# Three of eight chunks of an attention output projection's second half as seven block products instead of eight

## The chip, the cores and the metric

The kernel runs on one core of one Trainium2 chip. The core has a matrix engine (TensorE, PE in the profile, with its weight loads in a row of their own, PEld), a vector engine (VectorE, DVE), a scalar engine (ScalarE, ACT), GpSimd (POOL) and SyncE (SP), which here only issues transfers. On-chip memory is SBUF; matrix products go to PSUM, which has eight banks of 128x512 float32 values. The metric is the device time of one execution in microseconds (us).

## The reference

The reference is a two-layer encoder for 256 positions of width 2048. Layer 0 mixes tokens with a gated MLP, layer 1 with latent attention; behind each mixer stands a gated MLP with a short convolution. After each of the four, `x = LayerNorm(ALPHA * x + sublayer(x))`. What matters here is the end of the attention:

```python
    k_nope, v = jnp.split(kv, [NOPE_DIM], axis=-1)
    o = chunk_causal_attention(q_nope, q_rope, k_nope, k_rope, v)
    return o.reshape(B, S, MLA_HEADS * V_DIM) @ w_out
```

Sixteen heads give `o` of 256x2048, and `w_out` is 2048x2048. The result is added to the layer's input and normalised, and the last gated MLP (`x @ w_up`, 2048 to 11008) follows.

## The kernel before

**Products of split numbers.** Every float32 operand is split into a high part, which the matrix engine takes as it is, and a low part, the rest. A block product of a 128x128 block of activations and a 128x512 block of weights is then three matmuls: high by high, low by high, high by low (`prod_b`, L359). The high part of a weight chunk is a cast on ScalarE (L125), the low part a subtraction on VectorE (L128).

**The feed.** `Feed` (L77) streams all weights in chunks of 128x2048 (1 MB) in the order of their use: one load on SP into one of three "raw" slots (`_load`, L88), the split (`_split`, L104), and then the products. `feed.next(splits, loads)` hands over the next chunk and writes down the splits of the next two or three chunks and the loads of two more. The split parts lie in 14 "big" slots of 128x2048 words, which also hold the residual (2 slots), the heads' outputs `oT` (4 slots, one for four heads) and, before, the keys. Six "side" slots hold the split queries (4) and the values (2) during the attention. Small tiles rotate through five slots "t2".

**Order.** The program is written in one order; a scheduler at compile time puts the instructions of each engine into a fixed order. It goes by the written order among those that are ready in its own model, and a tile gets a slot when one is free. An engine then runs its list in order.

**Eight and seven block products.** A chunk holds two blocks of 128 rows of the weights (j = 0, 1) by two column blocks of 512 (f = 0, 1), and the activations have two row blocks (b = 0, 1): eight block products, 24 matmuls. Many stages of the kernel do some of their chunks in another way: a form of Strassen's method with seven block products, 21 matmuls. It needs sums of the four weight blocks, sums of the four activation blocks, and a last combination of the accumulators:

- `_seven` (L131) splits such a chunk. It forms four running sums `ts` of the weight blocks with three additions on VectorE (L139, L140, L142), and splits both the weights (`wh`, `wl`, 1536 columns) and the sums (`th`, `tl`, 1536 and 512 columns). It takes five slots where the other form takes two. From chunk 96 on, which holds here, the next cast on ScalarE is ordered behind the last cast of the sums (`self.sums`).
- `combine` (L296) forms the four sums of the activations with four subtractions or additions (`turn`, L288), one cast and one subtraction (L302, L303).
- `Banks.seven` (L435) issues the seven products, three into the accumulators of the plain form (`DIRECT`) and four into banks of their own (`OWN`). A stage with such chunks needs eight banks.
- `Banks.rest` (L445) combines the own banks after the last seven chunk with one copy on ScalarE and four operations on VectorE; `ln.fold` (L655) then adds the four results to the residual, scaled by ALPHA. A later `ln.piece` (L661) adds the plain accumulators.

**The stretch around the change.** The attention runs head by head (`attend_a`: scores and softmax; `attend_b`: transposed probabilities; `attend_c`, L1174: output of a head, split into `oT`), interleaved with the first half (columns 0 to 1023) of the output projection, `mo0`. Four pieces of the residual and their statistics follow (L1230 to L1232). Then comes the second half, `mo1` (L1233 to L1245): eight chunks c = 0 to 7, all with eight products into four banks. The products of the last three chunks are put off (`SKEW`, `late`) and issued bank by bank in `end_mo` (L1247). `boundary` (L555) does that: after the two column blocks of b = 0 are done, it takes their pieces and the statistics, scales the residual and has PE transpose it (`ln.put`, L713) while PE still works at b = 1; the transposed and split residual `xhl` feeds the first products of the next gated MLP, `upf`.

Of the kernel before, what the change touches and what calls it, by code (L numbers as in the profile page):

```python
# [9 lines left out]
F32R = mybir.dt.float32r  # L10
# [5 lines left out]
P = 128  # L16
S = 256
# [27 lines left out]
SKEW = 3  # L45
# [5 lines left out]

U_PAIRS = [[0, 1, 5, 7, 2, 6, 3, 4]] + [[0, 1, 2, 5, 3, 7, 4, 6]] * 5
U_SEVEN = [(2, 3)] + [(2, 3, 4)] * 4 + [(2, 3)]

T1, T2 = 6, 5
SLOTS = {"big": 14, "raw": 3, "side": 6}
# [153 lines left out]
def trunk(ctx: ExitStack, tc: tile.TileContext, x, xT, gm_in, gm_wout, ffn_up, ffn_dn,  # L210
          ml_q, ml_kv, ml_b, ml_out, consts, w_sT, b_s, ropes, ln_rows, out):
    nc = tc.nc
# [10 lines left out]
    def slot(shape, name, dt=F32, tag="big"):  # L223
        return big.tile(shape, dt, tag=tag, name=name, bufs=SLOTS[tag])

    def bank(name):
        return ps.tile([P, 512], F32, tag="bank", name=name)

    def mm(o, l, r, start, stop):
        recent[0] = nc.tensor.matmul(o, l, r, start=start, stop=stop, skip_group_check=True)  # L230
        return recent[0]
# [12 lines left out]
    chunks, parked = [], []  # L244
# [4 lines left out]
    for g in range(6):  # L249
        for p in U_PAIRS[g]:  # L250
            i = 48 + 8 * g + p // 2
            w = gm_in[i : i + 5 : 4, :, p % 2 * 1024 : p % 2 * 1024 + 1024].rearrange("f p c -> p f c")
            chunks.append((w, 2048, "seven" if p in U_SEVEN[g] else "wide"))

# [15 lines left out]
    chunks += [(ml_q[i], 2048, "") for i in range(4)]  # L270
    chunks += [(ml_kv[i], 3 * KVR, "") for i in range(5)] + [(ml_kv[5, :, 0:KVR], KVR, "")]
    chunks += [(ml_b[i], 2048, "") for i in range(ml_b.shape[0])]
    chunks += [(ml_out[i], 2048, "") for i in range(ml_out.shape[0])]
    chunks += [(ffn_up[1, i], 2048, "") for i in range(n_up)]
    back(ffn_dn[1], NF_FF)

# [1 line left out]
    feed = Feed(nc, tc.keep_in_program_order, behind, order, big, dram, chunks)  # L278
# [9 lines left out]
    def turn(t, k1, k2):  # L288

        at = lambda k, b: k[:, b] if len(k.shape) == 3 else k[:, b * P : (b + 1) * P]  # L290
        tc.keep_in_program_order(nc.vector.tensor_tensor(t[:, 0], at(k1, 0), at(k1, 1), ALU.subtract))
        nc.vector.tensor_tensor(t[:, 1], at(k1, 1), at(k2, 1), ALU.subtract)
        nc.vector.tensor_tensor(t[:, 2], t[:, 1], at(k1, 0), ALU.subtract)
        nc.vector.tensor_tensor(t[:, 3], at(k2, 0), t[:, 2], ALU.add)

    def combine(name, o, k1, k2):  # L296


        t = tp.tile([P, 4, P], F32, tag="t2", name=f"xs{name}", bufs=T2)
        turn(t, k1, k2)  # L300
        o = o.rearrange("p (h s c) -> p h s c", h=2, s=4)
        nc.scalar.copy(o[:, 0], t)  # L302
        nc.vector.tensor_tensor(o[:, 1], t, o[:, 0].bitcast(F32), ALU.subtract)  # L303
        return [(o[:, 0, i], o[:, 1, i]) for i in (1, 2, 0, 3)]

    for j in range(4):
        t = slot([P, 4, S], f"xraw{j}", tag="side")
# [47 lines left out]
    def x_parts(xs, k, b):  # L355
        t = xs[k // 4]
        return (t[:, k % 4, b * P : (b + 1) * P], t[:, k % 4, S + b * P : S + (b + 1) * P])

    def prod_b(acc, parts, hi, lo, pieces, first, last):  # L359

        xh, xl = parts
        for f, (o, w) in enumerate(pieces):
            mm(acc[f][:, :w], xh, hi[:, o : o + w], first, False)
            mm(acc[f][:, :w], xl, hi[:, o : o + w], False, False)
            mm(acc[f][:, :w], xh, lo[:, o : o + w], False, last)
# [37 lines left out]
    OWN, DIRECT = ("p1", "q5", "p7", "p6"), ("q3", "p2", "e", "q4")  # L403
# [327 lines left out]
    halfp = [(0, 512), (512, 512)]  # L731
# [19 lines left out]
    for gi in range(6):  # L751

        acc = Banks(f"v{gi}", DIRECT if gi == 0 else OWN + DIRECT if gi % 2 else DIRECT + OWN)
        rest = (None,) * 4
        for c, p in enumerate(V_PAIRS[gi]):
            a = [[x_parts(xhl, 2 * p + j, b) for j in range(2)] for b in range(2)]
            got = feed.next()
# [8 lines left out]
            if gi == 0 and p in V_SEVEN[1]:  # L766
                x4 = xraw[p // 2]
                room = xc_room[len(xc) // 2][:, len(xc) % 2, :]
# [8 lines left out]
            if c == 7 and gi == 5:  # L777
                wTg = []
                for i in range(4):
                    t = tp.tile([P, 2, P], F32, tag="t1", name=f"wT{i}", bufs=T1)  # L780
# [4 lines left out]
        for i, (n, t) in enumerate(zip(DIRECT, rest)):  # L785
            o = vt[:, i // 2, (i % 2) * 512 : (i % 2) * 512 + 512]
# [66 lines left out]
    def turned(g, tiles):  # L853

        for i, t in enumerate(tiles):
            src = v[g][:, i // 2, i % 2 * 512 : i % 2 * 512 + 512]
            for j in range(4):
                nc.tensor.transpose(t[:, j * P : (j + 1) * P], src[:, j * P : (j + 1) * P], ident)
            nc.scalar.copy(src, t)
# [7 lines left out]
    for g in range(6):  # L867
        direct, own = (ub[4:], ub[:4]) if g % 2 else (ub[:4], ub[4:])
        acc = Banks(f"u{g}", DIRECT + OWN, direct + own)
        for c, p in enumerate(U_PAIRS[g]):  # L870
            a = [[x_parts(xhl, 2 * p + j, b) for j in range(2)] for b in range(2)]
            got = feed.next()
            if p in U_SEVEN[g]:
                acc.seven(a, xc[p], *got, turned=512, across=True)
                if p == U_SEVEN[g][-1]:
                    rest = acc.rest()
# [17 lines left out]
        for i, t in enumerate(rest):  # L894
            o = v[g][:, i // 2, i % 2 * 512 : i % 2 * 512 + 512]
            nc.vector.tensor_tensor(o, o, t, ALU.mult)

    ln = Norm(0, {})
    acc, end = down(NF_GM, pT, "wo", ln, acts, tiles=ub, beside=lambda: turned(5, ub[4:]))
# [66 lines left out]
    ln, acc, end = ffn(0, ln, acc, end, False)  # L966
# [61 lines left out]
    acc = [[bank(f"mkv{b}_{f}") for f in range(2)] for b in range(2)]  # L1028
    for c in range(6):
        hi, lo = feed.next()  # L1030
        for j in range(3 if c < 5 else 1):
            k = 3 * c + j
# [9 lines left out]
    for b in range(2):  # L1042
# [3 lines left out]
        t = tp.tile([P, 4, ROPE], F32, tag="t1", name=f"kr2_{b}", bufs=T1)  # L1046
# [18 lines left out]
    acc = [[bank(f"qr{b}_{f}") for f in range(2)] for b in range(2)]  # L1065
    for c in range(2):
        hi, lo = feed.next()
        for j in range(2):
            k = 2 * c + j
# [52 lines left out]
    oT = []  # L1122
# [51 lines left out]
    def attend_c(h):  # L1174
        if h % 4 == 0:
            oT.append(slot([P, 4, 512], f"oT{h // 4}", F32R))
        pts = probs.pop(h)
        o = bank(f"o{h}")
        c = slice(h * P, (h + 1) * P)
        mm(o[:, 0:S], vv[0][:, c], pts[:, 0:S], True, False)  # L1180
        mm(o[:, P:S], vv[1][:, c], pts[:, S : 3 * P], False, True)
        hi = oT[h // 4][:, h % 4, 0:S]
        nc.scalar.copy(hi, o[:, 0:S])
        nc.vector.tensor_tensor(oT[h // 4][:, h % 4, S : 2 * S], o[:, 0:S], hi.bitcast(F32), ALU.subtract)

    for hf in range(2):
        acc = [[bank(f"vv{hf}_{b}_{f}") for f in range(2)] for b in range(2)]
        for c in range(2):
            hi, lo = feed.next()
            for j in range(2):  # L1190

                k = 2 * c + j
# [7 lines left out]
        for b in range(2):  # L1200
            for f in range(2):
                c = slice(hf * 1024 + f * 512, hf * 1024 + (f + 1) * 512)
                nc.scalar.copy(vv[b][:, c], acc[b][f])


    ln = Norm(2, res)
    acc = [[bank(f"mo0_{b}_{f}") for f in range(2)] for b in range(2)]
    LAG = 4
    attend_c(0)
    for t in range(3, H + LAG):  # L1210
        k = t - LAG
        if k >= 0:
            if k % 2 == 0:
                hi, lo = feed.next()
            w = slice((k % 2) * 1024, (k % 2) * 1024 + 1024)
        if 3 < t < H:
            attend_a(t)
        if k >= 0:
            prod_b(acc[0], x_parts(oT, k, 0), hi[:, w], lo[:, w], halfp, k == 0, k == KD - 1)
        if t < H + 2:  # L1220
            attend_c(t - 2)
        if k >= 0:
            prod_b(acc[1][:1], x_parts(oT, k, 1), hi[:, w], lo[:, w], halfp[:1], k == 0, k == KD - 1)
        if t - 1 < H:
            attend_b(t - 1)
        if k >= 0:
            prod_b(acc[1][1:], x_parts(oT, k, 1), hi[:, w], lo[:, w], halfp[1:], k == 0, k == KD - 1)
    ln.begin()
    ln.prep()
    for b in range(2):  # L1230
        for f in range(2):
            ln.piece(b, f, acc[b][f])  # L1232
    acc = [[bank(f"mo1_{b}_{f}") for f in range(2)] for b in range(2)]  # L1233
    late = []
    for c in range(8):
        left = 7 - c
        hi, lo = feed.next(splits=2 if left > 5 else 3, loads=2)
        for j in range(2):
            k = 2 * c + j
            w = slice(j * 1024, (j + 1) * 1024)  # L1240
            if left < SKEW:
                late.append((hi[:, w], lo[:, w], k))
                continue
            for b in range(2):
                prod_b(acc[b], x_parts(oT, k, b), hi[:, w], lo[:, w], halfp, k == 0, False)  # L1245

    def end_mo(b, f):  # L1247
        for hi, lo, k in late:
# [3 lines left out]
    ln, acc, end = ffn(1, ln, banks, end_mo, True)  # L1252
# [99 lines left out]
```

## Time and profile before

| | |
|---|---|
| time, median of 3 runs | 2465.37 us (2465.03 to 2466.1) |
| span of the profiled execution | 2464.6 us |
| matmuls of the output projection | 384 (256 with `wh`, 128 with `wl`) |
| attention with the first half of the projection | about 1637 to 1706 us of the span |
| second half of the projection | about 1706 to 1750 us |
| first products of the next gated MLP | from 1750.58 us |

The span counts from the first to the last instruction, and is 0.8 us below the median of the runs. In the profile, "busy" for PE counts pipelined matmuls, so PE at 100% says that it hardly ever waits, not that it runs at its peak. A group row of the profile gives line, engine, operation, output and inputs by tile name, sizes, count, then busy time and the mean of one in ns, and the idle time in front of them. A row of the timeline gives start, duration (both us), engine, line, operation, tiles and count; a bracket at its end gives the engine's idle time before it and what ended that.

### The profile page before, as it was taken

Reading aid. Unit: us, or ns where it says so; the run is one execution under the profiler, and the core shown is the slowest. Engines: PE = TensorE matmul, PEld = TensorE weight load, DVE = VectorE, ACT = ScalarE, POOL = GpSimd, SP = SyncE. Lnnn points to the kernel's source line nnn. Section 1 sums busy time; section 2 is a strip of 40 time slices with the busy share of each in tenths; the row PEclk is TensorE's granted clock in tenths of the full one; section 3 lists DMA queues with packets and bytes.
Section 4 is the critical chain, followed back from the end, with each engine's and each line's share of the span. In section 5 each row is a group of like instructions: output and inputs, shape, how many; then the busy total and the mean of one; then the engine's idle time right before and its main releaser. Section 6 shows DMA issues by size and latency. Waiting matters only on the chain. (4 is left out here: it accounts for less than half of the span.)

```text
span 2464.6 us, 32483 instructions
## 1 busy us (share of the span) xinstructions
PE 2458.1 (100%) x12494; PEld 2091.3 (85%) x12494; DVE 2054.7 (83%) x2734; ACT 1459.3 (59%) x1967; POOL 104.2 (4%) x202
## 2 busy tenths in 40 slices
PE   9999999999999999999999999999999999999999
PEld 7888888888888888888888888988888888888887
DVE  7999999989897788778777997867598787878798
ACT  6666665566565666656554566665565665555453
POOL 0000000000000000000001000000000000000000
PEclk9999999999999999999999999999999999999999
DMA  7555666656665778778868885544478787777885
GB/s 291 202 208 205 226 204 202 205 188 205 222 212 198 241 282 314 300 279 300 322 218 318 301 301 182 184 170 156 172 269 309 275 305 304 295 265 278 299 324 201
DMA packets 116428, 611.94 MB, mean 248 GB/s; under 512 B 10648, under 2 KB 10912, under 8 KB 75184
## 3 DMA queue, kind: packets, MB, share of 16 engines
q1 hardware_dynamic: 90128, 462.47, 52.9%
q0 software_dynamic: 26144, 147.39, 15.8%
q8 instruction: 98, 1.61, 0.3%
q14 instruction: 58, 0.48, 0.1%
HBM read 544.75 MB, written 65.06 MB: 247 GB/s over the span
## 5 line engine op out<-in xcount | busy, mean ns | idle before, releaser
L128 DVE TENSOR_TENSOR wl<-raw,wh 128x1024 fp32r<-128x1024 f32 (+4 forms) x645 | 958.4, 1501 | 169.5 <-ACT wh L125 124.0
L125 ACT CAST wh<-raw 128x1024 fp32r<-128x1024 f32 (+4 forms) x645 | 809.0, 1278 | 356.8 <-PE up L230 80.7
L230 PE MATMUL up<-xhl,wh 128*128 128x512 f32 x2624 | 611.4, 390 | 0.0
L230 PEld LDWEIGHTS up<-xhl,wh 128*128 128x128 f32 x2624 | 487.4, 188 | 97.8
L230 PEld LDWEIGHTS up<-xhl,wl 128*128 128x128 f32 x2624 | 325.8, 192 | 6.4
L230 PE MATMUL up<-xhl,wl 128*128 128x256 f32 x2624 | 328.1, 283 | 0.0
L125 ACT CAST th<-ts 128x1536 fp32r<-128x1536 f32 (+1 forms) x138 | 142.5, 1052 | 110.9 <-DVE ts L135 80.3
L230 PE MATMUL ub<-wh,xhl 128*128 128x512 f32 x576 | 179.5, 393 | 0.0
L128 DVE TENSOR_TENSOR tl<-ts,th 128x1536 fp32r<-128x1536 f32 (+1 forms) x138 | 163.2, 1221 | 10.4 <-PE dn_p L230 3.4
L230 PEld LDWEIGHTS ub<-wh,xhl 128*128 128x128 f32 x576 | 108.1, 188 | 24.2 <-issue 1.9
L230 PE MATMUL ub<-wl,xhl 128*128 128x512 f32 x288 | 112.1, 389 | 0.0
L135 DVE TENSOR_TENSOR ts<-ts,raw 128x512 f32<-128x512 f32 x138 | 95.1, 689 | 1.4
L135 DVE TENSOR_TENSOR ts<-raw 128x1024 f32<-128x1024 f32 x69 | 84.3, 1221 | 6.1 <-PE ub L230 3.8
L230 PE MATMUL mo<-wh,oT 128*128 128x512 f32 x256 | 82.5, 401 | 0.0
L230 PE MATMUL v_q<-wh,xhl 128*128 128x512 f32 x224 | 70.7, 391 | 0.3 <-ACT wh L125 0.3
L230 PEld LDWEIGHTS ub<-wl,xhl 128*128 128x128 f32 x288 | 54.1, 188 | 11.3
L230 PE MATMUL v_p<-wh,xhl 128*128 128x512 f32 x192 | 59.9, 389 | 0.0
L230 PEld LDWEIGHTS mo<-wh,oT 128*128 128x128 f32 x256 | 45.5, 189 | 7.1
L230 PEld LDWEIGHTS v_q<-wh,xhl 128*128 128x128 f32 x224 | 42.0, 188 | 10.5 <-ACT wh L125 1.9
L230 PE MATMUL mo<-wl,oT 128*128 128x512 f32 x128 | 50.1, 391 | 0.0
L724 ACT ACTIVATE lny<-lnt,lncol 128x128 f32<-128x128 f32 x96 | 36.6, 472 | 15.6 <-PE lnt L720 15.5
L388 DVE TENSOR_TENSOR h_0a<-up,lo_0a 128x256 f32<-128x256 f32 x41 | 17.2, 421 | 33.0 <-ACT lo_0a L386 33.0
(1838 smaller groups left out, 4338.4 us busy)
## 6 DMA issues: line engine op xcount, KB each, us to landing
raw<-in_ffn_up_dram SPq DMA_DIRECT2D x172, 1024.0 KB, 7.0
raw<-in_gm_in_dram SPq DMA_DIRECT2D x93, 1024.0 KB, 5.3
raw<-in_ffn_dn_dram SPq DMA_DIRECT2D x68, 1024.0 KB, 7.2
raw<-in_gm_wout_dram SPq DMA_DIRECT2D x48, 1024.0 KB, 5.3
praw<-in_ffn_dn_dram POOLq DMA_DIRECT2D x16, 1024.0 KB, 13.9
keptth<-pth POOLq DMA_DIRECT2D x16, 1024.0 KB, 8.1
kepttl<-ptl POOLq DMA_DIRECT2D x16, 1024.0 KB, 8.8
fth<-keptth POOLq DMA_DIRECT2D x16, 1024.0 KB, 9.4
```

The costliest lines, as they stand in the source:

```text
L125: cast = self.nc.scalar.copy(hi, raw)
L128: self.nc.vector.tensor_tensor(lo, raw, hi.bitcast(F32), ALU.subtract)
L135: add = lambda o, a, b: self.nc.vector.tensor_tensor(o, a, b, ALU.add)
L230: recent[0] = nc.tensor.matmul(o, l, r, start=start, stop=stop, skip_group_check=True)
L388: nc.vector.tensor_tensor(h, acc[:, 0:S], lo, ALU.add)
L724: nc.scalar.activation(y[:, j], t[:, j * P : (j + 1) * P], AF.Identity, bias=lncol[:, o : o + 1], scale=lncol[:, g : g + 1])
```

## The change

The attention's second half of the output projection takes the seven-product form for its chunks c = 2, 3 and 4.

```diff
+MO_SEVEN = (2, 3, 4)
...
-    chunks += [(ml_out[i], 2048, "") for i in range(ml_out.shape[0])]
+    chunks += [(ml_out[i], 2048, "seven" if i - ml_out.shape[0] // 2 in MO_SEVEN else "") for i in range(ml_out.shape[0])]
...
         hi = oT[h // 4][:, h % 4, 0:S]
         nc.scalar.copy(hi, o[:, 0:S])
         nc.vector.tensor_tensor(oT[h // 4][:, h % 4, S : 2 * S], o[:, 0:S], hi.bitcast(F32), ALU.subtract)
+        if h // 2 in MO_SEVEN:
+            if not oraw:
+                oraw["room"] = slot([P, 2 * len(MO_SEVEN), S], "oraw", tag="side")
+            oraw[h] = oraw["room"][:, h - 2 * MO_SEVEN[0], :]
+            nc.scalar.copy(oraw[h], o[:, 0:S])
+            if h % 2:
+                combine_o(h // 2)
...
+    oraw, osum = {}, {}
+
+    def combine_o(c):
+
+        if not osum:
+            room = slot([P, 2, 8 * P], f"os{c}", F32R, "side")
+            last = slot([P, 8 * P], f"ot{c}", F32R, "side")
+            osum["room"] = [room[:, 0, :], room[:, 1, :], last]
+        osum[c] = combine(f"o{c}", osum["room"][MO_SEVEN.index(c)], *[oraw.pop(2 * c + j) for j in range(2)])
...
-    acc = [[bank(f"mo1_{b}_{f}") for f in range(2)] for b in range(2)]
     late = []
+    second = Banks("mo1", DIRECT + OWN)
     for c in range(8):
         left = 7 - c
-        hi, lo = feed.next(splits=2 if left > 5 else 3, loads=2)
-        for j in range(2):
-            k = 2 * c + j
-            w = slice(j * 1024, (j + 1) * 1024)
-            if left < SKEW:
-                late.append((hi[:, w], lo[:, w], k))
-                continue
-            for b in range(2):
-                prod_b(acc[b], x_parts(oT, k, b), hi[:, w], lo[:, w], halfp, k == 0, False)
+        got = feed.next(splits=2 if left > 5 else 3, loads=2)
+        if left < SKEW:
+            for j in range(2):
+                w = slice(j * 1024, (j + 1) * 1024)
+                late.append((got[0][:, w], got[1][:, w], 2 * c + j))
+            continue
+        a = [[x_parts(oT, 2 * c + j, b) for j in range(2)] for b in range(2)]
+        if c in MO_SEVEN:
+            second.seven(a, osum[c], *got)
+            if c == MO_SEVEN[-1]:
+                for j, t in enumerate(second.rest()):
+                    ln.fold(j // 2, 2 + j % 2, t)
+        else:
+            second.eight(a, *got)
+    acc = [[second.acc[DIRECT[2 * b + f]] for f in range(2)] for b in range(2)]
```

So the heads 4 to 9 are also copied unsplit (`oraw`), each pair of them is combined into the sums that a seven chunk needs (`osum`), the stage takes eight banks instead of four, and after chunk 4 the own banks are combined and folded into the residual. Chunks 0 and 1 keep eight products, in the order of `Banks.eight`; chunks 5 to 7 stay put off as before. No load and no store is added or removed.

## The prediction

> **What bounds the kernel now.** First the page: the share of each engine, and the clock.
>
> ```profile
> PE 2458.1 (100%) x12494; PEld 2091.3 (85%) x12494; DVE 2054.7 (83%) x2734; ACT 1459.3 (59%) x1967; POOL 104.2 (4%) x202
> PEclk9999999999999999999999999999999999999999
> ```
>
> PE hardly ever waits, and its clock is full throughout. So a matmul taken away shortens the run if nothing else becomes late. VectorE, at 83%, is the next. Then the windows around the change: the attention with the first half of the projection, the second half up to the first scaling of the residual, and the next gated MLP up to its last chunks of the up-projection.
>
> ```profile
> core 0: us, PE busy (x) PEld busy (x) DVE busy (x) ACT busy (x) POOL busy (x), PEclk, DMA share, GB/s
> 1637.00:1700.60 63.60, 63.56 (x357) 54.17 (x356) 47.34 (x134) 39.75 (x109) 0.00 (x0) 1.00 0.41 152
> 1700.60:1744.00 43.40, 43.40 (x193) 35.91 (x192) 27.27 (x31) 17.51 (x18) 0.00 (x0) 1.00 0.57 207
> 1780.00:2250.00 470.00, 470.00 (x2691) 415.50 (x2690) 377.04 (x546) 282.84 (x402) 27.57 (x49) 1.00 0.77 286
> ```
>
> PE is dense in all three. VectorE idles 43.40 - 27.27 = 16.1 us in the stretch that changes, ScalarE 25.9. Behind it PE stays dense, so what is won or lost at about 1750 us reaches the end. The timeline of PE gives the price of a matmul:
>
> ```profile
> 1714.32 0.62 PE L230 MATMUL mo<-wh,oT 128*128 128x512 f32 x2
> 1714.78 0.39 PE L230 MATMUL mo<-wl,oT 128*128 128x512 f32 x1
> 1715.00 0.62 PE L230 MATMUL mo<-wh,oT 128*128 128x512 f32 x2
> ```
>
> Three matmuls start every 0.68 us, so one costs 0.227 us; the 0.39 us of a row is its way through the pipeline.
>
> **The change part by part.**
>
> *Removed on PE.* Three chunks of 24 matmuls become 21: nine fewer, 9 x 0.227 = 2.04 us, 0.08% of 2465. No transposition or other PE work is added. This is all that the change can win directly.
>
> [...]
>
> *Added on VectorE in the second half.* Rows of the same work elsewhere in this kernel:
>
> ```profile
> L135 DVE TENSOR_TENSOR ts<-raw 128x1024 f32<-128x1024 f32 x69 | 84.3, 1221 | 6.1 <-PE ub L230 3.8 <-DMA raw<-in_gm_in_dram 0.9 <-PE wo_q L230 0.7
> L135 DVE TENSOR_TENSOR ts<-ts,raw 128x512 f32<-128x512 f32 x138 | 95.1, 689 | 1.4
> L128 DVE TENSOR_TENSOR wl<-raw,wh 128x1536 fp32r<-128x1536 f32 x69 | 121.0, 1754 | 3.7 <-PE v_q L230 2.4 <-PE dn_q L230 1.1
> L128 DVE TENSOR_TENSOR tl<-ts,th 128x1536 fp32r<-128x1536 f32 x69 | 121.1, 1755 | 10.4 <-PE dn_p L230 3.4 <-ACT th L125 3.4 <-PE v_p L230 1.9
> L128 DVE TENSOR_TENSOR tl<-ts,th 128x512 fp32r<-128x512 f32 x69 | 47.4, 687 | 0.0
> L451 DVE TENSOR_TENSOR dn01u<-dn_p,dn01p x1: 685/685/685, 1466.9 to 1466.9; 128x512 f32<-128x512 f32 x1
> L658 DVE SCALAR_TENSOR_TENSOR res<-res,dn01p x1: 684/684/684, 1466.3 to 1466.3; 128x512 f32<-128x512 f32 x1
> ```
>
> A seven chunk takes 1.22 + 2 x 0.69 + 1.75 + 1.76 + 0.69 = 6.80 us in six operations. Operations that follow each other overlap a little: the pairs of 1.22 us subtractions below take 2.36 us, so 0.08 less each. That leaves 6.3 us, where a plain chunk takes two steps of 1.14, 2.28. Three chunks: 3 x 4.0 = 12.1 us. The four combining operations and four folds add 8 x 0.61 = 4.8 us; the later pieces stay at 0.69. Together 16.9 us, against the 16.1 us that VectorE idles there. So VectorE turns from 63% busy to full.
>
> *Whether the weights come in time.* The casts before, on ScalarE:
>
> ```profile
> 1700.67 2.00 ACT L125 CAST wh<-raw 128x1024 fp32r<-128x1024 f32 x2
> 1706.18 2.00 ACT L125 CAST wh<-raw 128x1024 fp32r<-128x1024 f32 x2 [3.51 <-issue]
> 1711.62 2.00 ACT L125 CAST wh<-raw 128x1024 fp32r<-128x1024 f32 x2 [3.44 <-issue]
> 1717.02 3.90 ACT L125 CAST wh<-raw 128x1024 fp32r<-128x1024 f32 x4 [3.39 <-PE mo L230]
> ```
>
> They come 5.44 us apart, the 24 matmuls of a chunk: each waits for the slots that PE gives back. Counted back from the boundary, these are chunks 2, 3, 4 and 5. So chunk 2's split begins three chunks ahead of its products (which start at about 1716.8), and five slots instead of two come free in time: two at 1700.7, two at 1706.1, two at 1711.5. I get its last part done at about 1715.6, needed at 1719. Chunk 3 follows at about 1722 (needed 1724), chunk 4 at 1728 to 1729 (needed 1728.9), since VectorE needs 6.3 us a chunk and PE 21 x 0.227 = 4.8. The lead is used up just at chunk 4; the put-off chunks 5 to 7 (2.28 us each) then end at about 1736, some tenths behind PE. I take 0.3 us of waiting on PE, with 0 and 2 as the ends. What queues behind a waiting matmul is all of PE.
>
> *The boundary, where the cover is gone.* VectorE's rows there before:
>
> ```profile
> 1727.95 4.63 DVE L128 TENSOR_TENSOR wl<-raw,wh 128x1024 fp32r<-128x1024 f32 x4 [3.08 <-issue]
> 1734.42 2.36 DVE L128 TENSOR_TENSOR wl<-raw,wh 128x1024 fp32r<-128x1024 f32 x2 [1.84 <-ACT wh L125]
> 1737.64 0.69 DVE L666 SCALAR_TENSOR_TENSOR res<-res,mo 128x512 f32<-128x512 f32 x1 [0.86 <-PE mo L230]
> 1741.72 0.69 DVE L666 SCALAR_TENSOR_TENSOR res<-res,mo 128x512 f32<-128x512 f32 x1 [2.66 <-PE mo L230]
> 1743.80 0.16 DVE L351 RECIPROCAL lnrs<-lnrs_0q 128x1 f32<-128x1 f32 x1 [0.36 <-ACT lnrs_0q L349]
> 1744.00 1.00 DVE L679 TENSOR_SCALAR res<-res,lnmv,lnrs 128x512 f32<-128x512 f32 x2
> ```
>
> Each waited for PE; the first scaling is done at 1744.54. Now the splits of chunks 5 to 7, the combination, the folds and the splits of the first two chunks of the next MLP stand in front of these pieces. The overrun is 16.9 - 16.1 = 0.8 us, plus what idle cannot be filled (0.36 for the root on ScalarE, and waits for slots and banks): 0.4 to 3. So the scaling is done 1.2 to 3.8 us later, at 1745.7 to 1748.3. What hangs on it:
>
> ```profile
> 1745.84 0.60 PE L720 MATMUL lnt<-ident,res 128*128 128x128 f32 x4
> 1749.91 0.62 ACT L727 CAST xhl<-lny 128x512 fp32r<-128x512 f32 x1
> 1750.58 0.50 PE L230 MATMUL upf<-wh,xhl 128*128 128x512 f32 x1
> 1750.81 1.51 ACT L724 ACTIVATE lny<-lnt,lncol 128x128 f32<-128x128 f32 x4 [0.28 <-PE lnt L720]
> ```
>
> Transposes 0.60, four activations 1.51, cast 0.62 and the hand-overs make 2.8 us at least from scaling to the first `upf` product. That gives 1748.5 to 1751.1. PE alone would be there at 1750.58 - 2.04 + 0.3 = 1748.8. So of the 2.04 us between all and nothing is kept; in the middle, scaling at 1747.0 and `upf` at 1749.8, it is 0.8 us. I take off 0.3 for the second row block, whose pieces are late too: 0.5 us kept.
>
> *Added in the attention.*
>
> ```profile
> L291 DVE TENSOR_TENSOR xs<-xraw x4: 282/285/286, 33.8 to 44.4; 128x128 f32<-128x128 f32 x4
> L303 DVE TENSOR_TENSOR xc<-xs,xc x4: 685/686/691, 34.9 to 47.8; 128x512 fp32r<-128x512 f32 x4
> L302 ACT CAST xc<-xs x4: 609/621/621, 34.2 to 47.2; 128x512 fp32r<-128x512 f32 x4
> L1183 ACT CAST oT<-o x16: 357/373/415, 1636.1 to 1700.2; 128x256 fp32r<-128x256 f32 x16
> 1632.35 0.71 POOL L162 DMA_DIRECT2D praw<-in_ffn_dn_dram  x1 [97.48 <-PE sc L230]
> ```
>
> Three pairs of heads cost VectorE 3 x (4 x 0.285 + 0.686) = 5.5 us and ScalarE six copies of 0.37 and three casts of 0.62, 4.1 us. VectorE idles 63.60 - 47.34 = 16.3 us there, ScalarE 23.9, and the combinations fall on odd heads, between the splits of chunks. So I cost them at nothing; the cover is the softmax work of one head lying beside the products of others, and if it is gone the 5.5 us count. The new waits: side slots are short. The last row shows a transfer for the next MLP taking the slot of the first four queries as soon as PE has read them, so `oraw` waits for the second (one head later), the sums for the third and fourth. Behind these waits stand a PSUM bank of one head and one or two of the five "t2" slots, not PE's products; nothing needs the sums before about 1716. GpSimd's queue gets nothing. SP's queue keeps its transfers; a raw slot of a seven chunk comes free some 4 us later or more. The first load of the next MLP and the landing time of these loads:
>
> ```profile
> 1720.49 30.83 SPq L100 DMA_DIRECT2D raw<-in_ffn_up_dram  x6
> raw<-in_ml_out_dram SPq DMA_DIRECT2D x11, 1024.0 KB, 4.8
> ```
>
> The MLP's first load takes the slot that chunk 5 gives back, at about 1731 by the split times above instead of 1720.5, and lands at 1736; the second lands at about 1739. Both are needed at 1749.
>
> *The sum.* -2.04 on PE, +1.5 for the boundary late by VectorE: -0.5. The profiled span is 2464.6, the median 2465.37 (0.8 us outside the span or between runs); I apply the sum to the median: **2464.9 us**.
>
> **The rivals.**
>
> *VectorE packs well and all is kept: 2463.3.* Then the scaling is done by 1745.7. For it: similar stages (the `v`, `dn` groups above) run seven chunks with VectorE near full and PE dense. Against it: there they are spread between plain chunks, here three stand in a row and a chain on VectorE follows. This is also the most that can be won.
>
> *The boundary gets later than the whole saving: 2468.1.* The place is the first `upf` product. If the splits of both MLP chunks and a cast of 2.0 us on ScalarE go in front of the chain (before, such a cast stood inside it, between the first three activations and the fourth), then scaling at 1748.3 and 2.8 + 2.0 give 1753.1; that is 2.5 us later than before. It decides once the scaling ends later than 1747.8 (1750.58 - 2.8). With the second row block as late again 0.3, +2.8.
>
> [...]
>
> *The attention slows: 2470.9.* If VectorE's 5.5 us all fall into the chain from scores to probabilities, -2.04 + 5.5 = +3.5; with ScalarE's 4.1 too, +7.6; the middle is +5.5. It decides when a head's softmax is not done by its turn on PE. Against it: before, PE waits 0.04 us in 63.6.
>
> *The change does not do what it says.* Were the chunks still split plainly, nothing would change: 2465.4. The diff marks them, so this gets little.
>
> **How the numbers follow.** A measurement of this kernel tells about 0.2%, 4.9 us, from no change. The forecast (0.5 us kept, itself 2463.5 to 2466.5) gets 0.42, all kept 0.25, the late boundary 0.18, the attention 0.13, no effect 0.02. Nothing here reaches 4.9 us faster; I leave 0.03 for another order of the instructions chosen at compile time. Slower by over 4.9 us: most of half the attention's cases and a few of the late boundary's, 0.11. Within 0.2%: 0.86. The range runs from 2462.8 (all kept, and half a microsecond of order) to 2470.0, which takes in the late boundary with chunk 4 waiting its 2 us, and half of the attention's cases.
>
> **What would show it.** Right: 375 matmuls of the projection instead of 384; VectorE nearly without idle from 1702 to 1746; the last fold behind 1738 and the first scaling at 1746 to 1748; `upf` starting at 1748.5 to 1751; PE idle between the last of them and the first `upf`. All kept: `upf` at 1748.5 without a gap. Late boundary: `upf` after 1751, PE waiting for `xhl`. Attention: its last `o` product later than before, PE idle in front of `pt` or `o`. Wrong altogether: a difference that arises after 1780, where nothing was changed.

## The result, and the profile after

| | before | after |
|---|---|---|
| time, median of 8 runs | 2465.43 us (2465.03 to 2466.1) | 2472.19 us (2471.24 to 2472.76) |
| ratio, 95% interval | | 1.0027 (1.0018 to 1.0036) |
| span of the profiled execution | 2464.6 us | 2469.6 us |

The change makes the kernel 6.8 us slower, above the range of the prediction (2462.8 to 2470.0). Three executions of more than 5000 us (two in the experiments below, one of the kernel before) are left out of all medians. The two spans lie only 5.0 us apart. Two offsets account for the rest, at least roughly: in all the runs of the experiments below and of the kernel after, the time is some 1.75 us above the span (2471.34 us for the span of 2469.6), so the span of 2464.6 belongs to an execution of about 2466.3 us, 0.9 us above its median; the profiled execution after was 0.85 us below its own. What follows is read inside the two profiled executions, from the first product of the projection on, which starts 0.51 us earlier after. (Line numbers after are two higher up to the attention: the casts are L127, the subtractions L130, the matmuls L232, the pieces L666 and L668, the statistics L669, the scaling L681.)

First the busy line of the page after (the line of the granted clock is all nines, as before).

```profile
PE 2458.3 (100%) x12485; PEld 2092.0 (85%) x12485; DVE 2074.9 (84%) x2769; ACT 1468.0 (59%) x1980; POOL 104.3 (4%) x202
```

PE has nine matmuls fewer (12494 before), VectorE is 20.2 us busier. Nothing here tells where 6.8 us went: a slice of the clock line is 62 us long. The windows of the kernel after do (columns: window, length, then busy time and instructions of PE, its weight loads, VectorE, ScalarE, GpSimd, then the granted clock, DMA share, GB/s):

```profile
1637.00:1700.60 63.60, 63.56 (x355) 54.14 (x355) 52.61 (x149) 43.19 (x118) 0.71 (x1) 1.00 0.46 162
1700.60:1744.00 43.40, 43.40 (x193) 35.95 (x192) 41.06 (x46) 20.47 (x20) 0.00 (x0) 1.00 0.45 168
...
1747.20:1750.80 3.60, 0.05 (x1) 0.05 (x1) 3.60 (x9) 0.64 (x2) 0.00 (x0) 1.00 0.57 178
1750.80:1752.40 1.60, 1.59 (x8) 1.16 (x8) 1.44 (x4) 0.76 (x3) 0.00 (x0) 0.61 0.63 266
1752.40:1754.00 1.60, 0.00 (x0) 0.00 (x0) 0.00 (x0) 1.60 (x6) 0.00 (x0) 0.50 0.00 0
...
1756.00:1758.00 2.00, 2.00 (x6) 1.57 (x5) 0.71 (x2) 2.00 (x7) 0.00 (x0) 0.51 0.00 0
1758.00:1760.00 2.00, 2.00 (x12) 1.65 (x11) 1.96 (x5) 0.62 (x2) 0.00 (x0) 1.00 0.00 0
...
1780.00:2250.00 470.00, 470.00 (x2691) 415.48 (x2691) 377.06 (x546) 281.05 (x402) 27.60 (x49) 1.00 0.76 284
```

Up to 1744 PE is as dense as before. From 1747.2 to 1750.8 it does nothing, while VectorE works without a break, and so again from 1752.4 to 1754.0, while ScalarE does. And PE's clock is halved for a while: a mean of 0.61 over 1.6 us and of 0.51 over the last 2 puts the half clock from about 1751.15 to 1757.96, 6.8 us. Behind 1760 all is as before.

PE's timeline after shows the two waits (the bracket is PE's idle time ahead of the row and what ended it):

```profile
1636.95 0.63 PE L232 MATMUL mo<-wh,oT 128*128 128x512 f32 x2
...
1705.51 0.62 PE L232 MATMUL mo_q<-wh,oT 128*128 128x512 f32 x2
...
1746.76 0.39 PE L232 MATMUL mo_q<-wl,oT 128*128 128x512 f32 x1
1750.75 1.64 PE L722 MATMUL lnt<-ident,res 128*128 128x128 f32 x8 [3.61 <-DVE res L681]
1754.05 0.79 PE L232 MATMUL upf<-wh,xhl 128*128 128x512 f32 x1 [1.66 <-ACT xhl L729]
...
1775.99 1.09 PE L232 MATMUL up<-xhl,wh 128*128 128x512 f32 x4
```

The same points before, which the prediction did not quote:

```profile
1637.46 0.63 PE L230 MATMUL mo<-wh,oT 128*128 128x512 f32 x2
...
1706.16 0.62 PE L230 MATMUL mo<-wh,oT 128*128 128x512 f32 x2
...
1749.94 0.39 PE L230 MATMUL mo<-wl,oT 128*128 128x512 f32 x1
...
1770.81 1.09 PE L230 MATMUL up<-xhl,wh 128*128 128x512 f32 x4
```

These rows give the ledger, after against before:

| stretch of PE | before | after | difference |
|---|---|---|---|
| first half of the projection, with the attention | 68.70 | 68.56 | -0.14 |
| second half, first to last product | 43.78 | 41.25 | -2.53 |
| last product to the first `upf` (1750.58 before) | 0.64 | 7.29 | +6.65 |
| first `upf` to the first `up` | 20.23 | 21.94 | +1.71 |
| sum | | | +5.69 |

The saving is there, even 0.5 us more of it than the nine matmuls, most of that because four transpositions that stood between the products now stand behind them. It is lost behind the last product. VectorE's timeline after says to what:

```profile
1726.78 6.89 DVE L130 TENSOR_TENSOR wl<-raw,wh 128x1024 fp32r<-128x1024 f32 x6
...
1737.80 0.68 DVE L660 SCALAR_TENSOR_TENSOR res<-res,mo1u 128x512 f32<-128x512 f32 x1
1738.40 4.62 DVE L130 TENSOR_TENSOR wl<-raw,wh 128x1024 fp32r<-128x1024 f32 x4
1742.94 0.68 DVE L666 TENSOR_TENSOR res<-res,mo_q 128x512 f32<-128x512 f32 x1
...
1744.13 1.28 DVE L669 BATCH_NORM_STATS2 lnst<-res 128x6 f32<-128x512 f32 x2
1745.33 2.35 DVE L130 TENSOR_TENSOR wl<-raw,wh 128x1024 fp32r<-128x1024 f32 x2
1747.60 0.26 DVE L674 BATCH_NORM_AGGREGATE lnmv<-lnst 128x2 f32<-128x24 f32 x1
1747.78 0.63 DVE L666 TENSOR_TENSOR res<-res,mo_e 128x512 f32<-128x512 f32 x1
1748.32 0.67 DVE L666 TENSOR_TENSOR res<-res,mo_q 128x512 f32<-128x512 f32 x1
1748.91 0.69 DVE L669 BATCH_NORM_STATS2 lnst<-res 128x6 f32<-128x512 f32 x1
1749.52 0.14 DVE L353 RECIPROCAL lnrs<-lnrs_0q 128x1 f32<-128x1 f32 x1
...
1750.17 1.90 DVE L681 TENSOR_SCALAR res<-res,lnmv,lnrs 128x512 f32<-128x512 f32 x4
```

Read it from the end. The scaling, which PE waits for, starts at 1750.17, where it started at 1744.00 before. In front of it, in the order that was fixed at compile time, stand not only the combination and the folds (the last of them at 1737.80) and the splits of the MLP's first two chunks (L130, x4), but the split of the third (1745.33), which stands between the statistics of the first row block and their aggregate; and then two pieces and a statistic of the second row block, between the aggregate and the reciprocal. Before, the third split stood behind the scaling, and so did the first piece of the second row block:

```profile
1745.80 0.69 DVE L666 SCALAR_TENSOR_TENSOR res<-res,mo 128x512 f32<-128x512 f32 x1 [0.80 <-PE mo L230]
...
1748.60 2.36 DVE L128 TENSOR_TENSOR wl<-raw,wh 128x1024 fp32r<-128x1024 f32 x2 [0.60 <-ACT wh L125]
```

### The profile page after: what moved, and what is told of

Read it like the earlier page. It is cut to its first block, busy times and chain, and to the rows that moved or that the text cites. A ratio compares the mean times of both kernels' runs of the same rounds, so it can differ in the third digit from the quotient of the medians.

```text
span 2469.6 us, 32516 instructions
## 1 busy us (share of the span) xinstructions
PE 2458.3 (100%) x12485; PEld 2092.0 (85%) x12485; DVE 2074.9 (84%) x2769; ACT 1468.0 (59%) x1980; POOL 104.3 (4%) x202
## 3 DMA queue, kind: packets, MB, share of 16 engines
q8 instruction: 98, 1.61, 0.3%
## 5 line engine op out<-in xcount | busy, mean ns | idle before, releaser
L130 DVE TENSOR_TENSOR wl<-raw,wh 128x1024 fp32r<-128x1024 f32 (+4 forms) x642 | 955.5, 1503 | 162.5 <-ACT wh L127 117.8
L127 ACT CAST wh<-raw 128x1024 fp32r<-128x1024 f32 (+4 forms) x642 | 807.6, 1281 | 358.1 <-PE up L232 83.3
L232 PE MATMUL up<-xhl,wh 128*128 128x512 f32 x2624 | 611.3, 390 | 0.0
L232 PEld LDWEIGHTS up<-xhl,wh 128*128 128x128 f32 x2624 | 487.4, 188 | 97.8
L232 PEld LDWEIGHTS up<-xhl,wl 128*128 128x128 f32 x2624 | 325.8, 192 | 6.4
L232 PE MATMUL up<-xhl,wl 128*128 128x256 f32 x2624 | 328.1, 283 | 0.0
L127 ACT CAST th<-ts 128x1536 fp32r<-128x1536 f32 (+1 forms) x144 | 148.6, 1051 | 118.7 <-DVE ts L137 83.8
L130 DVE TENSOR_TENSOR tl<-ts,th 128x1536 fp32r<-128x1536 f32 (+1 forms) x144 | 169.9, 1218 | 11.4 <-ACT th L127 3.6
L232 PE MATMUL ub<-wh,xhl 128*128 128x512 f32 x576 | 179.4, 393 | 0.0
L232 PEld LDWEIGHTS ub<-wh,xhl 128*128 128x128 f32 x576 | 108.0, 188 | 24.3 <-issue 1.9
L232 PE MATMUL ub<-wl,xhl 128*128 128x512 f32 x288 | 112.1, 389 | 0.0
L232 PE MATMUL v_q<-wh,xhl 128*128 128x512 f32 x224 | 70.9, 392 | 0.0
L232 PEld LDWEIGHTS ub<-wl,xhl 128*128 128x128 f32 x288 | 54.1, 188 | 11.4
L232 PE MATMUL v_p<-wh,xhl 128*128 128x512 f32 x192 | 59.9, 389 | 0.0
L232 PEld LDWEIGHTS v_q<-wh,xhl 128*128 128x128 f32 x224 | 42.2, 189 | 9.6 <-ACT wh L127 0.8
L232 PE MATMUL upf<-wh,xhl 128*128 128x512 f32 x128 | 43.4, 413 | 1.7 <-ACT xhl L729 1.7
L154 DVE TENSOR_TENSOR praw<-praw 128x512 f32<-128x512 f32 x64 | 43.9, 685 | 0.6
L390 DVE TENSOR_TENSOR h_1a<-up,lo_1a 128x256 f32<-128x256 f32 x41 | 17.2, 419 | 31.6 <-ACT lo_1a L388 31.3
```

The costliest lines, as they stand in the source:

```text
L127: cast = self.nc.scalar.copy(hi, raw)
L130: self.nc.vector.tensor_tensor(lo, raw, hi.bitcast(F32), ALU.subtract)
L154: add = lambda o, a, b: pin(nc.vector.tensor_tensor(o, a, b, ALU.add))
L390: nc.vector.tensor_tensor(h, acc[:, 0:S], lo, ALU.add)
```

## The experiments

The theory: the time is set by what stands on VectorE ahead of the first scaling; every microsecond too much there is idle time of PE, and the half clock, which followed 3.61 us of it after, comes on top. Rivals: the price lies in the form itself here (sums made in the attention, eight banks, slots), or in three such chunks in a row, or PE's wait is for something else. All the times below are medians of 7 to 11 runs, with before at 2465.4 to 2465.6 on the same chips. The diffs are against the kernel after. The expectations call some runs by short names: `e1_two` (two chunks), `e6_third_late` (the third MLP split one step later), `e2_late_splits` (two MLP splits later) and `e3_fill` (eight matmuls of filler).

### Two chunks instead of three

```diff
-MO_SEVEN = (2, 3, 4)
+MO_SEVEN = (2, 3)
```

> Two seven chunks (2 and 3) instead of three. Theory (the loss is VectorE's list in front of the first scaling of the residual, and the half clock that PE's wait brings): VectorE has some 4.0 us less to do, the first scaling ends near 1746 instead of 1750.6, PE waits under 1 us, no half clock; 1.36 us of matmuls saved: 2464 to 2466.5. Rival (each seven chunk costs its share somewhere else, in slots, banks or in the attention): two thirds of +6.8, about 2470.

2464.8 us, ratio 0.9997 (0.9988 to 1.0007). The timelines of VectorE and PE of this kernel:

```profile
1733.82 6.90 DVE L130 TENSOR_TENSOR wl<-raw,wh 128x1024 fp32r<-128x1024 f32 x6
```

```profile
1750.31 0.50 PE L232 MATMUL upf<-wh,xhl 128*128 128x512 f32 x1 [0.32 <-ACT xhl L729]
```

The x6 are the splits of the projection's last chunk and of the MLP's first two; the third MLP chunk follows behind the scaling, which starts at 1743.96. PE waits 0.32 us and its clock is 1.0 throughout. So the form as such is not slow here: one chunk fewer, and the loss of 6.8 us is gone. (The median is 0.7 us below before, but the interval still holds no change.) The rival of a fixed price falls.

### The same three, one chunk earlier

```diff
-MO_SEVEN = (2, 3, 4)
+MO_SEVEN = (1, 2, 3)
```

> Chunks 1, 2 and 3 with seven products instead of 2, 3 and 4: the same amount of work, the combination and the folds one chunk (5 us) earlier, the splits of three MLP chunks still in front of the chain on VectorE. Theory: VectorE's list starts earlier, into its idle time at the end of the attention, by up to 4 us, so the scaling ends at 1747 to 1749 and PE waits 1 to 3 us: 2466 to 2470. Rival (place does not matter, only the form): 2472.

2471.55 us, ratio 1.0026 (1.0015 to 1.0036). A miss: I thought that an earlier combination would help. On VectorE of this kernel the third MLP chunk's split again stands ahead of the aggregate (1746.20), the scaling starts at 1750.81, and PE waits as before:

```profile
1751.34 1.97 PE L722 MATMUL lnt<-ident,res 128*128 128x128 f32 x8 [3.32 <-DVE res L681]
```

The mean clock over the span is 0.998, as after. The folds are done 2.4 us earlier, but a split of the projection's last chunks that stood ahead of them now stands behind them. So the place of the combination doesn't decide, as the rival said; how much stands ahead of the scaling is the same.

### Without the combination and the folds

The own banks' products are computed, but not combined and not added to the residual (eight operations on VectorE and a copy on ScalarE left out).

```diff
-            if c == MO_SEVEN[-1]:
-                for j, t in enumerate(second.rest()):
-                    ln.fold(j // 2, 2 + j % 2, t)
```

> All three seven-product chunks, but the combination of the own banks and the four folds are left out (the own products are computed and not used): one copy on ScalarE and eight operations, 4.8 us, less on VectorE ahead of the boundary; PE's work is the same. Theory that VectorE's list ahead of the scaling is the whole cause: scaling starts near 1745.4, the first upf product near 1749, no half clock, and 1 to 2 of the 2.04 us are kept: 2463.5 to 2465.3. Rival, that the sums in the attention, the eight banks or the slots cost the time: 2469 or more.

2463.76 us, ratio 0.9993 (0.9984 to 1.0002), 1.8 us below before. VectorE's scaling and PE's first `upf` of this kernel:

```profile
1744.57 1.00 DVE L681 TENSOR_SCALAR res<-res,lnmv,lnrs 128x512 f32<-128x512 f32 x2
1745.49 2.35 DVE L130 TENSOR_TENSOR wl<-raw,wh 128x1024 fp32r<-128x1024 f32 x2
```

```profile
1748.34 0.50 PE L232 MATMUL upf<-wh,xhl 128*128 128x512 f32 x1 [0.16 <-ACT xhl L729]
```

With 4.8 us less of work on VectorE the scaling starts 5.6 us earlier, the third MLP split goes back behind it, and of the 2.04 us on PE 1.8 arrive in the time. The sums in the attention, the eight banks, the slots and the splits for seven products are all still there. They cost nothing that shows, and three such chunks in a row are not slow in themselves. That puts the cause on the VectorE work ahead of the scaling. (The copy on ScalarE went too; it takes 0.57 us after, and ScalarE waits 2.48 us for a load soon behind it.)

### The third MLP chunk's split one step later

```diff
-        got = feed.next(splits=2 if left > 5 else 3, loads=2)
+        got = feed.next(splits=2 if left > 5 or left == 0 else 3, loads=2 if left else 3)
```

> All three seven-product chunks; only the split of the third MLP chunk (2.35 us on VectorE, 2.0 us on ScalarE) is written one step later, behind the boundary's first row block. Theory (what stands on VectorE ahead of the scaling counts, one for one): scaling starts near 1747.8 instead of 1750.2, PE's idle time falls to some 1.2 us, no half clock, so 2.35 + 1.7 less than the changed kernel: 2467.5 to 2468.8. Rival (the wait is for something else, such as the loads or the banks): 2471.5 or more. A third way, that the late split comes in front of the second row block's chain: 2469 to 2471.

2469.84 us, ratio 1.0018 (1.0009 to 1.0027): 2.3 us below the kernel after. The direction is the theory's, the size is not; the time lies where the third way had it, but for another reason. VectorE of this kernel:

```profile
1745.74 0.26 DVE L674 BATCH_NORM_AGGREGATE lnmv<-lnst 128x2 f32<-128x24 f32 x1
...
1747.01 0.69 DVE L666 TENSOR_TENSOR res<-res,mo_q 128x512 f32<-128x512 f32 x1 [0.46 <-PE mo_q L232]
...
1748.35 0.15 DVE L353 RECIPROCAL lnrs<-lnrs_0q 128x1 f32<-128x1 f32 x1
...
1748.64 1.85 DVE L681 TENSOR_SCALAR res<-res,lnmv,lnrs 128x512 f32<-128x512 f32 x4
```

Counted from the projection's first product (1636.74 here), the aggregate comes 1.65 us earlier than after, but the scaling only 1.32: the second row block's pieces stand ahead of the reciprocal as before, and one of them now waits 0.46 us for PE's very last product. PE's idle time falls to 2.20 us, and still the clock halves. Windows of this kernel:

```profile
1747.00:1749.10 2.10, 0.00 (x0) 0.00 (x0) 2.05 (x6) 0.29 (x1) 0.00 (x0) 1.00 0.07 27
1749.10:1750.30 1.20, 1.11 (x8) 0.83 (x8) 1.20 (x4) 0.37 (x2) 0.00 (x0) 1.00 0.00 0
1750.30:1752.30 2.00, 0.00 (x0) 0.00 (x0) 1.96 (x6) 2.00 (x7) 0.00 (x0) 0.66 0.00 0
```

Eight transpositions, 1.11 us, between two idle stretches of 2.20 and 2.06 us did not keep the clock up.

### Two MLP splits later

```diff
-        got = feed.next(splits=2 if left > 5 else 3, loads=2)
+        got = feed.next(splits=(1, 2, 3, 3, 3, 3, 2, 2)[left], loads=(4, 3, 2, 2, 2, 2, 2, 2)[left])
```

> Three seven chunks as in the change, but the splits of the second and third chunk of the next gated MLP are written down behind the boundary's pieces (at the taking of chunks 6 and 7 one and two splits fewer; the loads stay). Theory: 4.6 us of VectorE's work leave the front of the chain, the first scaling ends near 1745 to 1746, most of the 2.04 us is kept: 2463.3 to 2465.5. Rival (the amount of added VectorE work decides, not what stands in front of the chain; those splits are then missing right behind it): 2468 to 2472.

2466.80 us, ratio 1.0006 (0.9997 to 1.0016), between the two expectations. The scaling starts at 1744.60, and the clock stays at 1.0: of the 6.8 us lost, 5.4 are back. But PE still waits 1.61 us ahead of `upf`, and the two splits now stand ahead of the second row block. VectorE and PE of this kernel:

```profile
1752.57 4.63 DVE L130 TENSOR_TENSOR wl<-raw,wh 128x1024 fp32r<-128x1024 f32 x4 [0.26 <-ACT wh L127]
```

```profile
1757.34 0.51 PE L232 MATMUL upf<-wh,xhl 128*128 128x512 f32 x1 [0.96 <-ACT xhl L729]
```

The work is not gone, it is late in another place.

### PE kept busy in its idle time

Matmuls of no use are put between PE's last product and the transpositions. For that the first transpositions are written behind the last product, where the compiled order of the kernel after had them anyway; VectorE's order at the boundary stays as it was. The first try had eight of them.

```diff
+FILL = 8
...
-        ln.put(0, 0)
+        if ln.idx != 2:
+            ln.put(0, 0)
         ln.piece(1, fs[0], acc[1][fs[0]])
         end(1, fs[1])
+        if ln.idx == 2:
+            ln.put(0, 0)
...
+        if (b, f) == (1, 3):
+            junk = bank("junk")
+            for _ in range(FILL):
+                tc.keep_in_program_order(mm(junk, ident, cst[:, 0:512], True, True))
```

> The change with eight matmuls of no use (identity by constants, 0.45 us each) on PE between the last product of the projection and the first transposes, where PE waited 3.61 us. They shorten nothing on VectorE. Theory: PE's clock stays full, the wait for the chain stays; of the loss only what ran at half clock goes, 1.7 to 2.0 us: 2470.2 to 2470.6. If the clock costs nothing: 2472.2. If the clock is most of the loss: below 2468.

2473.7 us, ratio 1.0034 (1.0022 to 1.0045). The filler was twice as long as meant, as its row shows, and pushed the transpositions back by some 3 us, to 1753.63, so its median says nothing on the price of the clock. In the profiled execution the clock stayed at 1.0, but not in all: in four of the seven runs the mean clock over the span was 0.999. These four have a median of 2474.05 us, the three others 2472.08. The filler in the profiled execution:

```profile
1746.77 7.03 PE L233 MATMUL junk<-cst,ident 128*128 128x512 f32 x16
```

The second try had four (`FILL = 4`).

> All three seven-product chunks, plus four matmuls of no use (two passes each, 0.44 us a pass by e3_fill, so 3.5 us) in the place where PE idles 3.61 us ahead of the first transposition. Nothing on VectorE or ScalarE changes. Theory that PE's idle time brings the half clock and that the half clock costs by itself: the granted clock stays at 1.0, the first upf product stays at about 1754, and the time is 1.5 to 2.2 us below the changed kernel's, 2470.0 to 2470.7. Rival, that the half clock costs nothing because PE waits for the vector chain in that stretch anyway: 2471.7 to 2472.7.

2470.04 us, ratio 1.0019 (1.0010 to 1.0028), 2.15 us below the kernel after. PE of this kernel:

```profile
1746.77 3.60 PE L233 MATMUL junk<-cst,ident 128*128 128x512 f32 x8
1750.53 1.12 PE L726 MATMUL lnt<-ident,res 128*128 128x128 f32 x8 [0.17 <-DVE res L685]
1753.70 0.50 PE L233 MATMUL upf<-wh,xhl 128*128 128x512 f32 x1 [2.05 <-ACT xhl L733]
...
1773.90 1.09 PE L233 MATMUL up<-xhl,wh 128*128 128x512 f32 x4
```

The transpositions start 113.85 us after the first product of the projection (1636.68 here), as in the kernel after (113.80), so the vector chain is just as late. But the stretch from the first `upf` to the first `up` is 20.20 us, as before the change, where it was 21.94, and the transpositions take 1.12 us instead of 1.64. By the medians the half clock costs 2.15 us by itself, nearly a third of the loss; 1.74 of it stand between those two points of the traces. That is rather too little. The profiled execution, the fastest of the eleven, kept its clock, but in five others the mean clock over the span was 0.999: the filler did not always hold it, and no trace shows where it fell. The six runs at 1.000 have a median of 2469.2 us, 3.0 below the kernel after, the other five 2471.0. The rival, that PE waits there anyway, falls.

### What is the best that can be kept?

One chunk:

```diff
-MO_SEVEN = (2, 3, 4)
+MO_SEVEN = (2,)
```

> One seven-product chunk (chunk 2), all else as in the changed kernel: three matmuls less, 0.68 us; VectorE gets 4.0 + 4.8 us of work where it idled 16.1. Theory that the loss is only what overflows VectorE's idle time: all of it is kept, scaling not later than before, no wait of PE ahead of upf: 2464.7 to 2465.0 beside 2465.5. Rival, that the form has a fixed price here (eight banks, the combination, the order): 2466 or more.

2464.84 us beside 2465.43, ratio 0.9998 (0.9989 to 1.0006): by the medians 0.6 of the 0.68 us, which the interval can't tell from nothing. PE doesn't wait.

Two chunks, with the third MLP split later (the edits of the first and the fourth experiment together):

> Two seven-product chunks (2 and 3), and the split of the third MLP chunk written one step later. The most that can be won is 6 matmuls, 1.36 us, 2464.1. In e1_two 0.7 of it was kept and PE still waited 0.32 us ahead of upf. Theory: with 2.3 us less ahead of the scaling that wait goes, and the time is 2464.0 to 2464.6. Rival: the late split delays the second row block's chain, as in e2_late_splits (0.96 and 0.22 us of idle PE there): 2465 to 2466.

2464.05 us beside 2465.56, ratio 0.9995 (0.9986 to 1.0004). PE of this kernel goes from the last product to `upf` without a gap:

```profile
1748.77 0.39 PE L232 MATMUL mo_q<-wl,oT 128*128 128x512 f32 x1
1749.01 0.60 PE L722 MATMUL lnt<-ident,res 128*128 128x128 f32 x4
1749.36 0.71 PE L232 MATMUL upf<-wh,xhl 128*128 128x512 f32 x2
```

The medians differ by 1.5 us, where six matmuls are 1.36. The interval still holds 1: a gain of 0.06% is at the edge of what such runs can show.

Three chunks, with the third MLP split later and the second row block's half of the combination and folds (four operations) behind the first scaling:

```diff
...
+                u3, d = new("u3"), new("d")
+                order(nc.vector.tensor_tensor(u3, acc["p7"], self.u2, ALU.add), self.after)
+                order(nc.vector.tensor_tensor(d, self.w, acc["p7"], ALU.subtract), self.after)
+                return d, u3
...
         ln.scale(0, 1)
+        if ln.idx == 2:
+            ln.half()
...
```

> All three seven-product chunks with the third MLP chunk's split one step later, as in e6_third_late, and the second row block's half of the combination and its two folds (four operations, 2.45 us on VectorE) ordered behind the first row block's scaling. Theory (one for one): scaling starts near 1746.2 instead of 1748.6, the first upf product near 1749.9, no half clock, so 2.4 + 2.1 less than e6_third_late: 2465.0 to 2466.0, with up to 1 more if the second row block's chain is late as in e2_late_splits. Rival, that only the whole of the folds or the MLP's splits can be moved with profit: 2468 or more. It decides whether three chunks can be worth as much as two.

2466.1 us, ratio 1.0003 (0.9994 to 1.0012). The scaling starts at 1743.84, the clock stays at 1.0, but PE waits three times for what is late in turn, 1.8 us in all:

```profile
1749.07 0.50 PE L232 MATMUL upf<-wh,xhl 128*128 128x512 f32 x1 [1.05 <-ACT xhl L745]
...
1759.77 0.73 PE L232 MATMUL upf<-wh,xhl 128*128 128x512 f32 x2 [0.25 <-ACT wh L127]
...
1761.03 0.50 PE L232 MATMUL upf<-wl,xhl 128*128 128x512 f32 x1 [0.53 <-DVE wl L130]
```

No order that was tried lets three chunks pay. What is taken from in front of the first scaling is late somewhere behind it: the theory holds for all the work that VectorE has to do around the boundary, not only for what stands ahead of the scaling. VectorE has no room for the third chunk.

All kernels beside each other, in us from the first product of the projection in each trace, in order of the time:

| kernel | scaling starts | PE idle ahead of the first `upf` | first `upf` | half clock | median |
|---|---|---|---|---|---|
| three, no folds | 107.65 | 0.16 | 111.42 | no | 2463.76 |
| two, third split late | 106.20 | 0 | 111.91 | no | 2464.05 |
| two | 106.03 | 0.32 | 112.38 | no | 2464.80 |
| one | 105.72 | 0 | 112.36 | no | 2464.84 |
| before | 106.54 | 0 | 113.12 | no | 2465.43 |
| three, half the folds and third split late | 106.97 | 1.05 | 112.20 | no | 2466.10 |
| three, two splits late | 107.70 | 1.61 | 112.73 | no | 2466.80 |
| three, third split late | 111.90 | 2.20 + 2.06 | 115.61 | yes | 2469.84 |
| three, four matmuls of filler | 113.26 | 0.17 + 2.05 | 117.02 | not in this trace | 2470.04 |
| three, chunks 1 to 3 | 113.49 | 3.32 + 1.66 | 117.65 | yes | 2471.55 |
| after | 113.22 | 3.61 + 1.66 | 117.10 | yes | 2472.19 |

The eight-matmul filler is left out. In the kernels up to "before" the scaling starts within 107.7 us and PE waits at most 0.32; below that line the time rises with what PE idles or does to no use, and by some 2 us with the half clock. The start of the scaling alone doesn't sort them: with half the folds late it is as early as before, and PE waits behind it. (Executions of one kernel differ by 1.1 to 3.2 us from the lowest to the highest, so the last columns agree with each other only to that.)

## Why the prediction was wrong

**The saving on PE: right.** 375 matmuls of the projection, and 2.53 us less for the second half, of which nine matmuls are 2.04. The kernel without folds gained 1.8 in time, by the medians.

**The splits in time: right, with room.** In VectorE's timeline the last part of chunk 4 is done at about 1726.9, earlier than the 1728 to 1729 of the prediction, and PE does not wait in the second half (43.40 us busy of 43.40 in the window). The 0.3 us that I took were nothing.

**The attention: right.** VectorE got 5.3 us more there (52.61 against 47.34 in the window), and the first half of the projection took 0.14 us less, not more. The cover held. The rival of 2470.9 comes near the measured time by chance only; its mechanism has no part in it.

**The boundary: this is the step that failed.** The prediction let the end of the first scaling slip by 1.2 to 3.8 us: the overrun of 16.9 - 16.1 = 0.8 us, and 0.4 to 3 for idle time that can't be filled. It took `upf` at 1749.8. The first scaling ends at about 1750.7 after (1750.17 plus one of four), not by 1748.3, and `upf` starts at 1754.05.

Both terms of that slip were about right; a third one was missing. Counted from the first product of the projection, the scaling starts 6.68 us later. Ahead of it VectorE works 47.74 us after (1700.09 to 1750.17) and 27.27 before (1700.60 to 1744.00), 20.5 us more, and its idle time there falls from 16.1 to 2.3 us, most of what is left being three waits of 0.72, 0.49 and 0.96 us. The difference, 20.5 - 13.8, is the 6.7. Of the 20.5 us, 16.5 are the added work that the prediction had at 16.9. The other 4.0 are work that was in the kernel before and stood behind the scaling: the third MLP split (1745.33 to 1747.60, 2.27 us) and two pieces and a statistic of the second row block (1747.78 to 1749.52, 1.74 us). The prediction counted what the change adds, as if all else stayed where it was, and put this at nothing.

In the program, the third split is written ahead of the boundary in both kernels (with the taking of chunk 7), the pieces behind the first two scalings. The third split's cast on ScalarE came at 1747.52 before and at 1744.24 after; the pieces stand where the chain waits for ScalarE's root. That fits a scheduler that takes what is ready, but why the compiler put them so was not tried, only that removing or moving VectorE's work helps.

Two smaller terms: from the end of the scaling to `upf` 3.3 us passed (3.2 in the filler run), where the prediction had 2.8 at least; and the 0.3 for the second row block was nothing, since the stretch behind the first `upf` took 20.20 us in the filler run and 20.23 before. (Of the VectorE rows that the prediction shows there, only the two pieces waited for PE; that changes nothing in its sum.)

The rival "the boundary gets later than the whole saving" named the place, the order and the point of decision (1747.8) rightly. Its size was too small: it saw the splits of two MLP chunks and a cast of 2.0 us where there were three chunks and the second row block's pieces, and gave 2468.1. In VectorE's rows after, the reciprocal did not pass the piece and the statistic that stand in front of it: at 1749.52 it comes 1.34 us after its input was ready (ScalarE's root after, 1747.89 + 0.29):

```profile
1747.89 0.29 ACT L351 ACTIVATE lnrs_0q<-lnmv,epsc 128x1 f32<-128x1 f32 x1 [0.35 <-DVE lnmv L674]
```

**The clock: left out altogether.** No case of the prediction gave a price to idle time of PE beyond the time itself. It is 2.15 us by the medians of the filler experiment, and the range ended 2.2 us below the measured time. In the trace after, the clock halved 4.0 us after PE fell idle at 1747.15 and came back 6.8 us later, at 1757.96; in the profiled executions it did not halve after single waits of 1.61 or 2.07 us. With the third split one step later it halved too, though 1.11 us of transpositions lay between the waits of 2.20 and 2.06 us. What sets the 4.0 and the 6.8 us was not shown.

**The loads.** The MLP's first loads were late enough for ScalarE to wait for them, 2.48 and 0.59 us, but its casts were done at 1736 and 1738.6, ahead of VectorE's turn at 1738.40 or beside it; that cost nothing that shows.

## What to carry to other kernels

Where an engine is to be filled to its last idle microsecond ahead of a chain of dependent steps, the sum of work against idle time is not enough: ask what else will be ready by then and will stand in front of the chain in a fixed order, and count that at its full length. Idle time of PE can cost more than itself: here the half clock that followed 3.61 us of it cost 2.15 us on top, by the medians of the filler experiment. And a saving that is linear in the number of chunks may have a cost that is not: by the medians, one of these chunks, or two with the third MLP split moved, keep about 0.7 us each, and the third costs 7.

## What the runs showed of the hardware

- PE's clock halved behind an idle stretch of 3.61 us (after, for 6.8 us), behind one of 3.32 us (chunks 1 to 3, a mean clock of 0.998 over the span), and with stretches of 2.20 and 2.06 us and 1.11 us of transpositions between (third split late, a mean of 0.66 over the 2.00 us from 1750.30); in the profiled executions it stayed at 1.0 with a single wait of 1.05, 1.61, 2.05 or 2.07 us. But of the two kernels with the last two waits, 5 of 11 and 4 of 7 executions had a mean clock of 0.999, so the same kernel can lose it in one execution and keep it in the next. What decides it is left open.
- The fillers' matmuls, of two plain float32 operands with 512 columns, show as two records each: 8 for 4 matmuls, 3.60 us in all, and 16 for 8, 7.03 us. That is a record every 0.43 us, with 0.60 us for the last, against 0.227 us for a matmul of the rounded kind that the kernel uses. That is why the first filler was twice as long as meant.
